# A decoder step on one Trainium2 core: norms between blocks summed tile by tile, a fixed order at the block boundaries, and x loaded in four parts

## Chip, cores and metric

The kernel runs on one core of one Trainium2 chip, as one program. The metric is the device time of one execution in microseconds. A profiled execution gives the trace. Engines are named as in the profile: PE (TensorE), DVE (VectorE), ACT (ScalarE), POOL (GpSimd), SP (SyncE, which only issues transfers here).

## What is computed

One inference step of a trunk of two layers. Layer 1 mixes time by an RWKV-7 recurrence, layer 2 by an RG-LRU; a causal convolutional FFN follows each. There are 256 prompt positions of one sequence and 8 sample positions with states of their own. Each of the four blocks is wrapped in the same way:

```python
h = rms_norm(x, norm_g_in) * (1 + sc) + sh        # sc, sh, gt: from the condition c, by silu(c) @ w_mod
out = mixer_or_ffn(h)
x = x + gt * rms_norm(out, norm_g_out)            # rms_norm: over the 2048 channels
```

After a block, the norm of `out` needs the sum of squares over all 2048 channels of `out`, and the next block's first products need the norm of the new x as well. The returned values are y and the updated states.

## The kernel before

Activations lie with channels on the partitions: 2048 channels are 16 chunks of 128 partitions, by T = 264 columns (256 prompt, 8 sample). `U0` holds x, `U1` a block's output. Weights are streamed from HBM in tiles of 1 MB (`raw`, `rawx`, five buffers), each of two pieces. ACT rounds a piece to its high half `wh` (L434), DVE subtracts to get the low half `wl` (L435); there are four buffers of each. A product is three matmuls (L455 high x high, L456 high x low, L457 low x high); a piece has 24 of them, four column blocks by two chunks by three (`mm_pieces`, L448). `mm_group` (L462) runs the pieces of a group of four column blocks. Between pieces it pumps the adaLN modulation (`wm_pump`, `wm_load`: small products of `w_mod` tiles, L345) as filler on PE.

**Norm of a block's output.** Each column block's result is squared on ACT (L530) and twelve of the sixteen squares are added on POOL into `sqacc`; the last four stay separate in `SqAcc.tail`. After the last product `rstd_of` (L480) multiplies a matrix of constants with `sqacc` and the four tails on PE (L484, five matmuls), ACT takes the root (`sd`, L486), DVE the reciprocal (`rs`, L488).

**Boundary between blocks** (`residual` L539, `residual_and_h` L554, called three times). The residual is a step per pair of chunks, `step(e, j, n)`: an engine multiplies U1 by the reciprocal (`bt`, L549) and adds to U0 (L550). The 8 sample columns of all chunks go in one pair of instructions (L543, L544). From the new U0 the kernel forms `x * (1 + sc)` in a high half `XH` (ACT, L580) and a low half `XL` (DVE, L581); the sample and shift columns are prepared in `xe` (POOL, L568) and cast in one piece (L569, L570). ACT also squares the new x by pairs (`sqb`, L577), DVE adds the pair (L582), PE sums them (`norm(p)`, L586). The first products of the next block, `main(p)` for the eight pairs of chunks p = 0 to 7, run on XH and XL ahead of that norm, which is divided out later. Pairs 0 to 4 have their step on DVE, 5 to 7 (chunks 10, 12, 14) on POOL. The engines' order here is that of the tile framework's scheduler.

**Start.** x comes in one transfer (L326). `NormPipe.push` squares each chunk on ACT and sums it on PE; eight chunks are pushed after the first modulation piece, eight after the second (L751 to L756). Then come the transposed modulation vector, the first h and the projections of the RWKV mixer.

**WKV stage.** The recurrence runs by chunks of 16 positions; its 1749 jobs are issued in the order of a table, `ORDER` (L37), under `manual_schedule`.

**Tail** (L1789 to L1794). The last residual is done in steps on DVE and POOL, then eight output transfers are issued.

Of the kernel before, what the change touches and what calls it, by code (L numbers as in the profile page):

```python
# [8 lines left out]
F32 = mybir.dt.float32  # L9
# [33 lines left out]
v1 2v0 v1 2s2 2w4 p6 p7 b3 p6 2w5 u4 u5 x1 p6 v1 p6 2v0 2v1 2b2 v0 3q0 d4 b3 v1 q0 2b3 2q0 p7 3b3 q0 2p8 2h0
d4 2p7 p6 2h0 q0 p8 h0 3q0 l8 p8 2p6 b4 4s2 p6 3q0 3b3 p7 s4 p7 2v1 d5 2x2 p7 2l9 3q0 2v2 p7 2v1 p7 q0 h0 v1
2v2 a0 q0 o0 2p6 3p7 w7 2o0 2p6 l11 v3 2p7 2q1 v2 d7 q1 v2 4p9 p8 o0 2h0 2s4 2v2 2q1 v2 2b4 b5 o0 2v2 2p8 v3
a1 3o0 l10 h0 p7 v3 2x2 p9 q0 x2 v3 s4 w6 2s4 4o0 p9 3x2 p8 2x2 w6 p8 2q1 2p8 b4 d6 4q1 b4 2g0 s4 2g0 2p9 3g0
u6 w7 u7 v3 2q1 b4 2g0 3q1 s4 g0 v4 b4 2v4 l10 4v3 d6 d7 2w8 2s6 u8 v4 b4 v3 4q1 2g0 2a0 w9 q0 q1 a0 v3 a0 s6
# [241 lines left out]
def build(nc, tc, I, O, dbg=None):  # L289
# [42 lines left out]
    def pv(name, i, n=1):  # L332
# [1487 lines left out]
```

## Time and profile before

| | |
|---|---|
| median of 3 runs | 2849.76 us (2849.45 to 2850.34) |
| the profiled execution's own time | 2848.57 us |
| its span in the trace | 2846.8 us |
| mean granted clock of PE | 0.987 |
| busy: PE, DVE, ACT, POOL | 96%, 62%, 48%, 18% |

Times in the trace count from the start of the span. A granted clock of 1.00 is the higher level of 2.4 GHz. In a timeline each row has the start, the length, the engine, the line, the operation and, in brackets, how long the engine was idle before it and which instruction released it. The stages: start to 40 us, projections to 378, WKV stage to 712, its output product to 813, boundary 1, FFN, boundary 2 from 1670, RG-LRU mixer, boundary 3 from 2021, FFN, tail from 2824.

### The profile page before, as it was taken

Reading aid. Unit: us, or ns where it says so; the run is one execution under the profiler, and the core shown is the slowest. Engines: PE = TensorE matmul, PEld = TensorE weight load, DVE = VectorE, ACT = ScalarE, POOL = GpSimd, SP = SyncE. Lnnn points to the kernel's source line nnn. Section 1 sums busy time; section 2 is a strip of 40 time slices with the busy share of each in tenths; the row PEclk is TensorE's granted clock in tenths of the full one; section 3 lists DMA queues with packets and bytes.
Section 4 is the critical chain, followed back from the end, with each engine's and each line's share of the span. In section 5 each row is a group of like instructions: output and inputs, shape, how many; then the busy total and the mean of one; then the engine's idle time right before and its main releaser. Section 6 shows DMA issues by size and latency. Waiting matters only on the chain.

```text
span 2846.8 us, 61582 instructions
## 1 busy us (share of the span) xinstructions
PE 2740.7 (96%) x25820; PEld 2526.2 (89%) x25820; DVE 1753.7 (62%) x2824; ACT 1358.7 (48%) x2187; POOL 524.4 (18%) x1045
## 2 busy tenths in 40 slices
PE   7999999888999999999999999999999999999997
PEld 6899876665989999999999989999899999999997
DVE  5877776876476535545545579775765455455555
ACT  5333435644455434433434459785554444344444
POOL 2111435553121000000000023332210000000002
PEclk9999999999999999999999999999999999999998
DMA  8777558776766666666666665666666555555552
GB/s 330 288 261 244 185 176 246 241 234 215 276 237 232 257 245 238 252 252 255 247 237 252 256 248 199 253 239 237 237 244 252 207 180 178 178 180 184 183 183 76
DMA packets 146566, 648.48 MB, mean 228 GB/s; under 512 B 41152, under 2 KB 60752, under 8 KB 78064
## 3 DMA queue, kind: packets, MB, share of 16 engines
q1 hardware_dynamic: 145216, 641.25, 62.7%
q8 instruction: 202, 3.31, 0.5%
q0 software_dynamic: 1072, 3.30, 0.4%
q14 instruction: 76, 0.62, 0.1%
HBM read 629.42 MB, written 15.07 MB: 226 GB/s over the span
## 4 chain that ended last, share of the span: by engine, by line
PE 86%; DVE 7%; ACT 2%; DMA 2%; issue 1%; POOL 1%; SPq 0%; DVEq 0%; ACTq 0%; POOLq 0%
PE bk L455 18%; PE bk L456 18%; PE bk L457 18%; PE sq L455 7%; PE sq L456 7%; PE sq L457 7%; PE wm L345 5%; DVE wl L435 1%; PE bk L902 1%; ACT wh L434 1%; DVE bt L549 1%; PE bk L908 1%; PE bk L814 0%; PE sq L814 0%; DVE U L550 0%
## 5 line engine op out<-in xcount | busy, mean ns | idle before, releaser
L435 DVE TENSOR_TENSOR wl<-raw,wh 128x1024 fp32r<-128x1024 f32 x444 | 547.6, 1235 | 495.0 <-ACT wh L434 485.8
L434 ACT CAST wh<-raw 128x1024 fp32r<-128x1024 f32 x444 | 464.5, 1048 | 631.6 <-PE bk L456 428.4
L455 PE MATMUL bk<-AH,wh 128*128 128x264 f32 x2352 | 670.6, 285 | 1.4 <-ACT wh L434 1.4
L457 PE MATMUL bk<-AH,wl 128*128 128x264 f32 x2352 | 669.1, 284 | 1.7 <-DVE wl L435 1.6
L456 PE MATMUL bk<-AL,wh 128*128 128x264 f32 x2352 | 668.6, 284 | 0.8 <-DVE AL L493 0.8
L435 DVE TENSOR_TENSOR wl<-rawx,wh 128x1024 fp32r<-128x1024 f32 x310 | 379.3, 1226 | 331.9 <-ACT wh L434 326.8
L434 ACT CAST wh<-rawx 128x1024 fp32r<-128x1024 f32 x310 | 324.4, 1048 | 452.9 <-PE bk L456 332.7
L455 PE MATMUL bk<-ah,wh 128*128 128x264 f32 x1786 | 514.6, 289 | 9.2 <-ACT ah L492 5.5
L457 PE MATMUL bk<-ah,wl 128*128 128x264 f32 x1786 | 510.6, 286 | 0.5 <-DVE wl L435 0.5
L456 PE MATMUL bk<-al,wh 128*128 128x264 f32 x1786 | 510.6, 286 | 0.0
L455 PEld LDWEIGHTS bk<-AH,wh 128*128 128x128 f32 x2352 | 443.3, 188 | 20.7 <-ACT cv L1560 8.4
L457 PEld LDWEIGHTS bk<-AH,wl 128*128 128x128 f32 x2352 | 441.7, 188 | 2.8 <-DVE wl L435 2.8
L456 PEld LDWEIGHTS bk<-AL,wh 128*128 128x128 f32 x2352 | 442.5, 188 | 1.0 <-DVE AL L493 1.0
L455 PEld LDWEIGHTS bk<-ah,wh 128*128 128x128 f32 x1786 | 337.6, 189 | 27.6 <-ACT wh L434 8.1
L457 PEld LDWEIGHTS bk<-ah,wl 128*128 128x128 f32 x1786 | 338.1, 189 | 1.4 <-DVE wl L435 0.8
L456 PEld LDWEIGHTS bk<-al,wh 128*128 128x128 f32 x1786 | 338.4, 189 | 0.6 <-DVE al L493 0.2
L455 PE MATMUL sq<-AH,wh 128*128 128x264 f32 x1040 | 296.7, 285 | 0.1
L456 PE MATMUL sq<-AL,wh 128*128 128x264 f32 x1040 | 295.6, 284 | 0.0
L457 PE MATMUL sq<-AH,wl 128*128 128x264 f32 x1040 | 295.4, 284 | 0.0
L1553 POOL COPY fgs<-gt 128x10 f32<-128x10 f32 x88 | 53.4, 634 | 1307.5 <-ACT gt L1547 1286.2
L455 PEld LDWEIGHTS sq<-AH,wh 128*128 128x128 f32 x1040 | 196.0, 188 | 9.6 <-ACT cv L1560 3.4
L456 PEld LDWEIGHTS sq<-AL,wh 128*128 128x128 f32 x1040 | 195.7, 188 | 0.0
(469 smaller groups left out, 4501.3 us busy)
## 6 DMA issues: line engine op xcount, KB each, us to landing
raw<-in_wst SPq DMA_DIRECT2D x224, 1024.0 KB, 4.9
rawx<-in_wst SPq DMA_DIRECT2D x157, 1024.0 KB, 4.8
raw<-in_wmr SPq DMA_DIRECT2D x72, 1024.0 KB, 7.6
raw<-in_wmr SPq DMA_DIRECT2D x88, 512.0 KB, 5.5
rawx<-in_wmr SPq DMA_DIRECT2D x44, 1024.0 KB, 8.2
raw<-in_wmq SPq DMA_DIRECT2D x23, 1024.0 KB, 4.9
rawx<-in_wmq SPq DMA_DIRECT2D x9, 1024.0 KB, 4.8
lu<-in_lup SPq DMA_DIRECT2D x32, 128.0 KB, 4.8
```

The source lines that it names most:

```text
L345: PE.matmul(ps[32 * g:32 * g + 32, :cols], cs[:, k0 + kk, :], raw[:, (kk * 4 + g) * cols:(kk * 4 + g + 1) * cols], start=(k0 + kk == 0), s ...
L434: S.copy(wh, t)
L435: V.tensor_sub(wl, t, wh.bitcast(F32))
L455: PE.matmul(ps[:, :n], h[:, kk, sl], xh, start=first and kk == 0, stop=False)
L456: PE.matmul(ps[:, :n], h[:, kk, sl], xl, start=False, stop=False)
L457: PE.matmul(ps[:, :n], l[:, kk, sl], xh, start=False, stop=last and kk == 1)
L549: e.tensor_tensor(t, U1[:, j:j + n, :TP], r1[:, None, :TP].to_broadcast([128, n, TP]), op=mult)
L902: PE.matmul(out[HH[(i + turn) % 2]], lhs[HH[i]], rhs[HH[i]], start=start, stop=stop, skip_group_check=True)
L908: PE.matmul(out[q], lhs(r), rhs[r], start=start, stop=stop, skip_group_check=True)
L1553: G.tensor_copy(gs[:, m], gt[:, TP:])
```

## The change

1. **Norm sums.** `rstd_of` is gone. `SqAcc` gets `begin` (the matmul of `sqacc`) and `add_tail`. In the last group of a block, `begin` is issued ahead of the last piece, and a hook after each column block of that piece squares it; the first two tails are added behind the third and fourth column blocks, so that one norm matmul lies between them. The gating of the last two column blocks (`acc.rest`) is moved behind the reciprocal.
2. **Filler.** In that last group two pieces of modulation filler are pumped ahead of the last piece, not behind it; at the boundary two, and two more after the fixed part.
3. **Boundary.** A fixed order (`manual_schedule`) up to `norm(0)`. The sample columns are split: two chunks on DVE, 14 on POOL; so are `xe` and its casts. Squares, halves and pair sums become calls of their own.
4. **Start.** x in four transfers; all sixteen squares are pushed ahead of the modulation pieces.
5. **Tail.** The eight steps are all on DVE, the sample columns on POOL, and each output transfer is issued behind its step.
6. **`ORDER`**: another order of the same jobs. Its first line was `s0 g0 p0 l0 2p0 p1 3x0 ...`, and is `l0 g0 2p0 s0 x0 g0 2x0 l0 6p0 l1 ...`.

```diff
-    SP.dma_start(U0[:, :, 1:], I["xT"])
+    for j in range(0, 16, 4):
+        SP.dma_start(U0[:, j:j + 4, 1:], I["xT"][:, j:j + 4])
...
+            end = q == nk // 2 - 1
+            if acc and end:
+                acc.begin()
+            mm_pieces(pss, pc, [rhs(2 * q), rhs(2 * q + 1)], q == 0, end, T, hook if end else None)
...
-                elif p == 0:
+                elif p == (2 * pace[0] - 1 if ahead and q >= nk // 2 - 2 else 0):
                     wm_pump(2, False)
-            if ahead and q == nk // 2 - 1:
-                for w in range(ahead):
-                    wm_load(wm_state["i"] + w)
+                    for w in range(ahead):
+                        wm_load(wm_state["i"] + w)
...
+        def begin(s):
+            s.ps = bank()
+            PE.matmul(s.ps[:, :T], onesd, s.acc, start=True, stop=False)
+
+        def add_tail(s, i):
+            PE.matmul(s.ps[:, :T], onesd, s.tail[i], start=False, stop=i == 3)
...
-        parts(0)
-        main(0)
-        step(V, 2, 2)
-        step(G, 12, 2)
-        parts(1)
-        norm(0)
-        step(V, 4, 2)
+        with tc.manual_schedule(engines=MANUAL):
+            step, sample = residual(pool, acc)
+            wm_pump(2, False)
+            wm_load(wm_state["i"])
+            wm_load(wm_state["i"] + 1)
+            sample(V, 0, 2)
+            sample(G, 2, 14)
+            step(V, 0, 2)
+            extra(V, 0, 2)
+            halves(0)
+            main(0)
+            step(V, 2, 2)
+            extra(G, 2, 14)
+            halves(1)
+            squares(0)
+            main(1)
+            pairsum(0)
+            step(V, 4, 2)
+            squares(1)
+            pairsum(1)
+            step(G, 10, 2)
+            step(G, 12, 2)
+            norm(0)
+        wm_pump(2, False)
         parts(2)
-        main(1)
         norm(1)
         step(V, 6, 2)
         step(G, 14, 2)
...
+    for j in range(16):
+        np0.push(U0[:, j, 1:])
     for kp in range(4):
         mod_piece(0, kp)
-        if kp < 2:
-            for j in range(8 * kp, 8 * kp + 8):
-                np0.push(U0[:, j, 1:])
...
+            def hook(m, ps):
+                acc.push(ps[:, :T])
+                if m < 2:
+                    gated(m, ps)
+                else:
+                    acc.rest.append(lambda: gated(m, ps))
+                    acc.add_tail(m - 2)
+
+            if g == 3:
+                with tc.manual_schedule(engines=MANUAL):
+                    mm_group(16, rhs, bgg, 2, acc, hook)
+                    acc.add_tail(2)
+                    acc.add_tail(3)
+                break
...
-    step = residual(bp, acc, 8)
-    for e, j in ((V, 0), (G, 12), (V, 2), (V, 4), (G, 14), (V, 6), (V, 8), (V, 10)):
-        step(e, j, 2)
-    for j in (0, 2, 12, 4, 6, 8, 14, 10):
-        SP.dma_start(O["yT"][:, j:j + 2], U0[:, j:j + 2, 1:])
+    with tc.manual_schedule(engines=MANUAL):
+        step, sample = residual(bp, acc, 8)
+        sample(G, 0, 16)
+        for j in range(0, 16, 2):
+            step(V, j, 2)
+            SP.dma_start(O["yT"][:, j:j + 2], U0[:, j:j + 2, 1:])
```

`mm_group(16, ...)` is the form in the out-projection; the FFN's last group has the same hook with the addition to the partial sums in front.

How the instructions move is shown at boundary 1 (the other two are alike). Line numbers of the changed kernel are its own: L435 and L436 are there the casts wh and wl, L456 to L458 the products, L523 and L526 the norm sums, L547 the reciprocal, L560 and L561 a step, L584 and L585 XH and XL, L579 the squares, L595 the pair sums.

On PE, before, at the end of the out-projection (the last products of a piece, the filler, the norm sums, more filler, and the first product of main(0)):

```order
L455 MATMUL bk<-ah,wh 128x264
L456 MATMUL bk<-al,wh 128x264
L457 MATMUL bk<-ah,wl 128x264
L345 MATMUL wm<-raw,cT 32x512 x8
L484 MATMUL sq<-sqacc,onesd 128x264
L484 MATMUL sq<-sq,onesd 128x264 x4
L345 MATMUL wm<-rawx,cT 32x512 x4
L345 MATMUL wm<-raw,cT 32x512 x12
L455 MATMUL sq<-XH,wh 128x274
L456 MATMUL sq<-XL,wh 128x274
```

Now, ahead of the last piece:

```order
L346 MATMUL wm<-raw,cT 32x512 x8
L523 MATMUL sq<-sqacc,onesd 128x264
L456 MATMUL bk<-ah,wh 128x264
L457 MATMUL bk<-al,wh 128x264
L458 MATMUL bk<-ah,wl 128x264
```

and at the end of that piece:

```order
L456 MATMUL bk<-ah,wh 128x264
L457 MATMUL bk<-al,wh 128x264
L458 MATMUL bk<-ah,wl 128x264
L526 MATMUL sq<-sq,onesd 128x264 x3
L346 MATMUL wm<-rawx,cT 32x512 x4
L346 MATMUL wm<-raw,cT 32x512 x12
L456 MATMUL sq<-XH,wh 128x274
L457 MATMUL sq<-XL,wh 128x274
```

Eight filler matmuls of the program now stand ahead of the last piece, with the sum of `sqacc` behind them; of the four tails three are left behind the last product.

On DVE, before, from the last wl cast ahead of the reciprocal up to the first XL and pair sums (the next wl cast, the one for main(4), stands eleven rows further):

```order
L435 TENSOR_TENSOR wl<-rawx,wh 128x1024
L1509 TENSOR_TENSOR U_10834<-bk,mod_7071 128x8
L488 RECIPROCAL rs_11694<-sd 128x264
L543 TENSOR_TENSOR f_11696<-U_10834,rs_11694 128x128
L549 TENSOR_TENSOR bt<-U_10834,rs_11694 128x512
L544 TENSOR_TENSOR U_78<-U_78,f_11696 128x16x8
L550 TENSOR_TENSOR U_78<-U_78,bt 128x2x256
L549 TENSOR_TENSOR bt<-U_10834,rs_11694 128x512
L570 TENSOR_TENSOR XL<-xe,XH 128x16x18
L550 TENSOR_TENSOR U_78<-U_78,bt 128x2x256
L581 SCALAR_TENSOR_TENSOR XL<-U_78,mod_11379,XH 128x256 x2
L582 TENSOR_TENSOR sqb<-sqb 128x264 x2
```

Now, from XL 0 and 1 (eight rows behind the reciprocal) up to the pair sum ahead of XL 4 and 5:

```order
L585 SCALAR_TENSOR_TENSOR XL<-U_78,mod_11382,XH 128x256 x2
L436 TENSOR_TENSOR wl<-rawx,wh 128x1024
L560 TENSOR_TENSOR bt<-U_10837,rs_11703 128x512
L561 TENSOR_TENSOR U_78<-U_78,bt 128x2x256
L591 TENSOR_TENSOR XL<-xe,XH 128x14x18
L585 SCALAR_TENSOR_TENSOR XL<-U_78,mod_11382,XH 128x256 x2
L436 TENSOR_TENSOR wl<-rawx,wh 128x1024
L595 TENSOR_TENSOR sqb<-sqb 128x264
L560 TENSOR_TENSOR bt<-U_10837,rs_11703 128x512
L436 TENSOR_TENSOR wl<-rawx,wh 128x1024
L561 TENSOR_TENSOR U_78<-U_78,bt 128x2x256
L595 TENSOR_TENSOR sqb<-sqb 128x264
```

Three wl casts, for main(2), main(3) and main(4), now stand between the steps; before, two of them were ahead of the reciprocal.

On ACT, before, from the root to the casts for main(4) and main(5):

```order
L486 ACTIVATE sd<-sq,epsn 128x264
L580 ACTIVATE XH<-U_78,mod_11379 128x256
L569 CAST XH<-xe 128x16x18
L577 ACTIVATE sqb<-U_78 128x528
L580 ACTIVATE XH<-U_78,mod_11379 128x256 x2
L577 ACTIVATE sqb<-U_78 128x528
L580 ACTIVATE XH<-U_78,mod_11379 128x256 x5
L577 ACTIVATE sqb<-U_78 128x528
L580 ACTIVATE XH<-U_78,mod_11379 128x256 x2
L577 ACTIVATE sqb<-U_78 128x528
L580 ACTIVATE XH<-U_78,mod_11379 128x256 x2
L434 CAST wh<-rawx 128x1024 x2
```

Now, from the sample columns' XH:

```order
L590 CAST XH<-xe 128x2x18
L584 ACTIVATE XH<-U_78,mod_11382 128x256 x2
L435 CAST wh<-rawx 128x1024
L590 CAST XH<-xe 128x14x18
L584 ACTIVATE XH<-U_78,mod_11382 128x256 x2
L579 ACTIVATE sqb<-U_78 128x528
L435 CAST wh<-rawx 128x1024
L579 ACTIVATE sqb<-U_78 128x528
L435 CAST wh<-rawx 128x1024 x2
L584 ACTIVATE XH<-U_78,mod_11382 128x256 x3
L579 ACTIVATE sqb<-U_78 128x528
L584 ACTIVATE XH<-U_78,mod_11382 128x256 x5
```

The wh casts for main(2) to main(5) are now ahead of XH 4 and 5, which stand in the last row behind XH 10 to 12; before, XH 4 and 5 were ahead of the casts.

## Rows read from the trace of the kernel before

**Rows 1.** Windows by stage: PE, PEld, DVE, ACT, POOL busy; clock; DMA; GB/s.
```profile
378.00:712.00 334.00, 294.44 (x5876) 209.34 (x5875) 237.21 (x555) 171.53 (x456) 157.52 (x350) 0.96 0.76 235
712.00:2824.00 2112.00, 2089.07 (x16933) 1990.50 (x16933) 1228.71 (x1755) 1032.69 (x1484) 261.87 (x512) 0.99 0.61 224
```

**Rows 2.** Chain of waits, 0 to 45 us: start, length, engine, tile, line.
```profile
1.67 12.45 DMA U<-in_xT
...
25.71 1.28 ACT L511
...
29.24 0.16 DVE wmtt L740
...
33.99 1.25 PE bk L455 x4
```

**Rows 3.** Timeline of PE, start.
```profile
22.74 3.83 PE L506 MATMUL bk<-sq,onesd 128*128 128x264 f32 x16
...
27.39 1.06 PE L345 MATMUL wm<-rawx,cT 128*32 128x128 f32 x32
```

**Rows 4.** Windows of 2 us, start.
```profile
22.00:24.00 2.00, 2.00 (x38) 1.64 (x27) 0.00 (x0) 0.75 (x3) 0.00 (x0) 1.00 1.01 418
```

**Rows 5.** Timeline of PE, boundary 1.
```profile
812.89 0.28 PE L457 MATMUL bk<-ah,wl 128*128 128x264 f32 x1
813.10 1.92 PE L345 MATMUL wm<-raw,cT 128*32 128x512 f32 x16
...
815.51 1.94 PE L484 MATMUL sq<-sq,onesd 128*128 128x264 f32 x8
...
825.37 0.59 PE L455 MATMUL sq<-XH,wh 128*128 128x274 f32 x1 [2.74 <-ACT XH L580]
827.94 0.60 PE L456 MATMUL sq<-XL,wh 128*128 128x274 f32 x1 [1.97 <-DVE XL L581]
...
832.82 0.48 PE L455 MATMUL sq<-XH,wh 128*128 128x274 f32 x1
...
836.76 0.48 PE L455 MATMUL sq<-XH,wh 128*128 128x274 f32 x1
```

**Rows 6.** Windows of 4 us, boundary 1, and their sum.
```profile
824.00:828.00 4.00, 0.66 (x2) 0.35 (x2) 4.00 (x5) 2.20 (x5) 2.86 (x2) 0.58 1.01 426
...
sum 24.00, PE 17.89 PEld 13.84 DVE 21.96 ACT 12.09 POOL 9.51; mean PE 2.98 PEld 2.31 DVE 3.66 ACT 2.02 POOL 1.59
```

**Rows 7.** Timeline of DVE, boundary 1.
```profile
814.21 1.23 DVE L435 TENSOR_TENSOR wl<-rawx,wh 128x1024 fp32r<-128x1024 f32 x1 [0.76 <-PE wm L345]
...
818.00 1.80 DVE L488 RECIPROCAL rs<-sd 128x264 f32<-128x264 f32 x1 [2.49 <-ACT sd L486]
...
820.05 1.75 DVE L549 TENSOR_TENSOR bt<-U,rs 128x512 f32<-128x512 f32 x1
...
822.91 0.68 DVE L550 TENSOR_TENSOR U<-U,bt 128x512 f32<-128x512 f32 x1
...
832.09 1.51 DVE L581 SCALAR_TENSOR_TENSOR XL<-U,mod,XH 128x256 fp32r<-128x256 f32 x1
...
834.87 0.87 DVE L581 SCALAR_TENSOR_TENSOR XL<-U,mod,XH 128x256 fp32r<-128x256 f32 x2
```

**Rows 8.** Timeline of POOL, boundary 1.
```profile
819.88 1.37 POOL L549 TENSOR_TENSOR bt<-U,rs 128x512 f32<-128x512 f32 x1 [28.50 <-DVE rs L488]
```

**Rows 9.** Timeline of ACT, boundary 1.
```profile
833.82 0.89 ACT L580 ACTIVATE XH<-U,mod 128x256 fp32r<-128x256 f32 x2
834.61 1.04 ACT L434 CAST wh<-rawx 128x1024 fp32r<-128x1024 f32 x1
```

**Rows 10.** Timeline of PE, boundary 2.
```profile
1685.42 0.60 PE L456 MATMUL sq<-XL,wh 128*128 128x274 f32 x1 [1.97 <-DVE XL L581]
```

**Rows 11.** Timeline of DVE, tail.
```profile
2829.66 1.80 DVE L488 RECIPROCAL rs<-sd 128x264 f32<-128x264 f32 x1 [1.29 <-ACT sd L486]
...
2842.75 0.69 DVE L550 TENSOR_TENSOR U<-U,bt 128x512 f32<-128x512 f32 x1
```

More of the change, by code (lines that the diff above doesn't have):

```diff
@@ L43 @@
[L43 to L47, printed above, removed]
@@ L446, in build, with mm_pieces @@
     ws = Stream()
-    def mm_pieces(pss, pc, rhs2, first, last, n=T):
+    def mm_pieces(pss, pc, rhs2, first, last, n=T, hook=None):
         h, l = pc
@@ L539, in residual, with sample @@
     def residual(pool, acc, nb=2):
-        r1 = rstd_of(pool, [acc.acc] + acc.tail, "rs1")
+        sd = pool([128, T], F32, "sd", 1)
+        S.activation(sd, acc.ps[:, :T], AF.Sqrt, bias=epsn)
+        r1 = pool([128, T], F32, "rs1", 1)
+        V.reciprocal(r1, sd)
+        for f in acc.rest:
+            f()
         f8 = pool([128, 16, 8], F32, "f8", 1)
-        V.tensor_tensor(f8, U1[:, :, TP:], r1[:, None, TP:].to_broadcast([128, 16, 8]), op=mult)
-        V.tensor_tensor(U0[:, :, TP + 1:], U0[:, :, TP + 1:], f8, op=add)
+        def sample(e, j, n):
+            x = U0[:, j:j + n, TP + 1:]
+            e.tensor_tensor(f8[:, j:j + n], U1[:, j:j + n, TP:], r1[:, None, TP:].to_broadcast([128, n, 8]), op=mult)
+            e.tensor_tensor(x, x, f8[:, j:j + n], op=add)
         def step(e, j, n):
@@ L550, in step @@
             e.tensor_tensor(x, x, t, op=add)
-        return step
+        return step, sample
     def residual_and_h(acc, sc, sh, AH, AL):
@@ L581, in parts, with extra, pairsum @@
                 V.scalar_tensor_tensor(XL[:, j, :TP], x, sc[:, j, 0:1], XH[:, j, :TP].bitcast(F32), op0=mult, op1=sub)
-            V.tensor_tensor(q[:, 0], q[:, 0], q[:, 1], op=add)
-            sqs[p] = q
+        def extra(e, j, n):
+            x = slice(j, j + n)
+            e.tensor_tensor(xe[:, x, :8], U0[:, x, TP + 1:], sc[:, x, 1:], op=mult)
+            S.copy(XH[:, x, TP:], xe[:, x])
+            V.tensor_sub(XL[:, x, TP:], xe[:, x], XH[:, x, TP:].bitcast(F32))
+        def pairsum(p):
+            q = sqs[p]
+            V.tensor_tensor(q[:, 0], q[:, 0], q[:, 1], op=add)
+        def parts(p):
+            squares(p)
+            halves(p)
+            pairsum(p)
+        pss = [bank() for _ in range(4)]
+        ms = bank()
         def norm(p):
@@ L1506, in out_proj @@
             for m in range(4):
[L1507 to L1509 removed]
+                gated(m, pss[m])
         return acc
@@ L1572, in ffn, with gated, hook @@
                     S.activation(junk, acc.acc[:, :1], AF.Sqrt)
-                pss = mm_group(b - a, lambda k: hid[k], None, 2 if last and g == 3 else 0)
+                def gated(m):
+                    u = U1[:, 12 + m]
+                    S.activation(u[:, :TP], u[:, :TP], AF.Copy, scale=gate[:, 12 + m, 0:1])
+                    V.tensor_tensor(u[:, TP:], u[:, TP:], gate[:, 12 + m, 1:], op=mult)
+                def hook(m, ps):
+                    u = U1[:, 12 + m]
+                    V.tensor_tensor(u, u, ps[:, :T], op=add)
+                    acc.push(u)
+                    if m < 2:
+                        gated(m)
+                    else:
+                        acc.rest.append(lambda: gated(m))
+                        acc.add_tail(m - 2)
+                if last and g == 3:
+                    with tc.manual_schedule(engines=MANUAL):
+                        mm_group(b - a, lambda k: hid[k], None, 2, acc, hook)
+                        acc.add_tail(2)
+                        acc.add_tail(3)
+                    break
+                pss = mm_group(b - a, lambda k: hid[k])
                 for m in range(4):
```

115 lines of the change are left out of this document (54 added, 61 removed).

## The prediction

> **What bounds the kernel now.** I read the busy times by stage first, then the waits of TensorE (PE), then the timelines of the stretches that the change touches. The windows by stage show that from 712 us to 2824 us PE is busy 2089.07 of 2112.00 us, and in the stage before it, the WKV recurrence, 294.44 of 334.00 us [rows 1]. So a reordering off PE's path can gain nothing; it can only close PE's gaps or open new ones. The gaps that this change can reach are four: the start, up to the first weight product; the three boundaries between blocks, where the kernel normalises a block's output and prepares the next input; the last boundary, which is the tail; and the 39.6 us that PE idles in the WKV stage.
>
> At the start the chain of waits shows one transfer of x lasting 12.45 us, later the Sqrt table, then the modulation's transpose at 29.24 and the first product at 33.99 [rows 2]. PE's timeline shows why the middle takes so long: the norm's 32 matmul records are interleaved with the modulation products, the last 16 taking 3.83 us from 22.74, so that the fourth modulation piece runs only at 27.39 [rows 3].
>
> At boundary 1 the last product starts at 812.89, the norm sums end around 817.4, the first product of the new block starts at 825.37 and the second, which needs the low half XL, at 827.94 [rows 5]. VectorE (DVE) finishes the reciprocal at 818.00 + 1.80 = 819.80 [rows 7]; I call this moment R and count from it. Product groups have 24 matmuls each; group main(2) starts at 836.76 = R + 16.96, and PE no longer waits there [rows 5]. Boundary 2 has the same wait of 1.97 us for XL [rows 10], and boundary 3 the same pattern.
>
> **The norm sum: no earlier R.** The five norm matmuls take 2.4 us in all (two records each, from 815.02 to 817.45), so 0.48 each. Two of the five now run before the end of the last group, and the square of the third column block lies under the products of the fourth. But the modulation filler of 16 records, 1.9 us, which stood between the last product and the sums, is moved ahead of the last piece too [rows 5]. PE therefore ends its last product 1.94 + 0.96 = 2.90 us later than before, and what follows is a square (0.39), the last tail, the root (0.48) and the reciprocal (1.80): with the hand-overs about 3.55 us. R falls 6.45 us after the old end of the products, against 819.80 - 813.17 = 6.63 before. Gain 0.2 us per boundary. Two gated copies move behind the root on ScalarE (ACT) and hide under the reciprocal.
>
> **From R to main(2): the new fixed order.** main(0) gets what it needs sooner: DVE now does a sample part of two chunks, one step, and goes straight to XL 0 and 1, so main(0) starts near R + 4.7, not R + 8.1. That is worth something only if main(1) and main(2) follow, and I price main(2), since PE runs without a wait from there.
> DVE's own work up to XL 4 and 5, at durations that nothing disturbs (0.65 for an instruction of a step, 0.43 for an XL, 1.23 for a wl cast [rows 7], and about 0.42 for a pair sum): before, 0.6 for the sample part, 0.45 for its XL, eight step instructions 5.2, seven XL 3.0 and three pair sums 1.26, 10.5 us in all. It was there at 834.87 + 0.87 = R + 15.9 [rows 7]: 5.4 us were lost while GpSimd (POOL) worked. The rows show the loss: a 0.65 instruction took 1.75 at 820.05, beside a POOL step of 1.37 [rows 8], and an XL took 1.51 at 832.09 [rows 7].
> After: copies and sample part 0.7, seven step instructions 4.55, six XL 2.6, the sample's xe and XL 0.75, three pair sums 1.26, and three wl casts 3.7: 13.5 us. The casts are the difference. Before, the casts for main(2) and main(3) were done ahead of R (the last at 814.21, when DVE waited anyway [rows 7]); the new order puts them, and main(4)'s, between the steps. POOL still has three steps (10, 12, 14) and a sample part of 14 chunks, so I keep the loss at 5.4 us and add 0.6 us for waiting on ACT's first XH and wh: XL 5 at R + 19.5, main(2) from about R + 19.2. Against R + 16.96 that is 2.2 us later, 2.0 with the earlier R.
> ACT gives a second, lower bound. Its casts for main(4) and main(5) wait until PE has read main(0) and main(1), and XH 4 and 5 stand behind them, and behind XH 10 to 12, which wait for POOL. With 1.04 for a cast and 0.45 for an XH [rows 9], main(2) comes some 3.8 us (a cast, five XH, a square of 0.55) after main(1) ends, at R + 4.7 + 4.4 + 3.0 = R + 12.1: R + 15.9. DVE's bound is later and decides.
> PE idles some 5 us ahead of main(2). Gaps of 2.74 and 1.97 us [rows 5] came with a granted clock of 0.58 from 824 to 828 [rows 6], so mostly the lower of the two levels, 1.2 GHz: main(0) with one norm took 832.82 - 827.94 = 4.88 us, main(1) with two took 3.94 [rows 5]; less 0.48 a norm, 4.4 against 3.0, so 1.4 us were lost, say 1.5. I add it once more, since the new gap is longer than each of those. **Per boundary +3.5 us**; bounds -2.7 (rival 1) and +7.5 (rival 2). The moved POOL sample part, the DMA issues of two modulation tiles and the filler's two later pieces I cost at nothing: DVE's steps cover them, and PE's queue has wm records ready before main(0). Without that cover the filler costs its 1.9 us.
> The Trainium skill (SBUF — State Buffer, section "SBUF: two separate sides") says that VectorE with two SBUF inputs and GpSimd hold a shared port pair exclusively, the loser blocking for the whole instruction; the trace agrees, with 1.75 us for what takes 0.65 alone.
>
> **The start.** x comes in four loads, and its squares and sums stand ahead of the modulation products. The last byte of x lands no sooner than 14.14; then four squares and their sums are left, and table load, root and reciprocal end near 20, off the path. The end is now set by the modulation tiles: four of 1 MB behind x at 418 GB/s [rows 4] take 9.9 us, up to 24.0; the last products, 1.06 [rows 3], end near 25.1, the transpose starts there in place of 29.24, and the 4.75 us from there to the first product stay [rows 2]. **-4.1 us**; bounds -5.5 (transfers overlap better) and -2.5 (the added loads delay the tiles by 1.6 us, as chosen).
> The Trainium skill (SBUF — State Buffer, "The DMA setup-cost knee") advises the largest single transfer, since each pays about 2 us; by it three more loads would take back the start's gain. The DMA share beside several loads in flight was 1.01 [rows 4], which speaks against that.
>
> **WKV stage.** The table is another order of the same 1749 jobs, and two ACT table loads (1.28 us each, as the one at 25.71 [rows 2]) fall away. No row says what PE gains or loses in its 39.6 us of gaps. I take 0; bounds -5 and +5, an eighth of the gaps.
> **Tail.** R moves 0.4 us later against the old end of the products, as the sums are no longer preceded by filler; eight DVE steps of 1.2 us and two disturbed starts take 11.4 us, where DVE and POOL together took from 2831.47 to 2843.44 [rows 11]. **-0.2 us**; bounds -1 and +0.6. Outputs leave step by step, but the last still ends the kernel.
> **Sum.** 3 x 3.5 - 4.1 + 0 - 0.2 = +6.2 us on the profiled execution's 2848.57: 2854.8. That execution is 1.19 us under the runs' median, 2849.76, so the forecast in medians is 2856.0.
>
> **Rivals.** 1. *POOL's interference falls into DVE's waits for ACT.* Then DVE is not the bound, PE has no long gap, and its clock stays up: main(0) and main(1) take 3.0 us each from R + 4.7, main(2) follows 3.8 us later at R + 14.5: -2.5, with R -2.7. Three times, with the start and the tail: -12.4, 2837.4: faster. For it: DVE does wait at two points. Against: from 816 to 840 DVE was busy for 21.96 of 24 us [rows 6], so it has little waiting to give.
> 2. *Every POOL instruction costs DVE its full length.* Six step instructions at 1.4 us [rows 8] and short ones of 1 us in all, 9.4 us in place of 5.4: XL 5 at R + 23.5, +7.5 per boundary, +18.2 in all: 2868.0. For it: the 1.75 and 1.51 above show losses of 1.1. Against: before, 9.51 us of POOL [rows 6] cost 5.4. By the skill's rule of the exclusive lock this is the case to expect.
> 3. *R really comes earlier*, because the filler would have waited for its tiles: -1.9 per boundary, +0.5 in all: 2850.3.
> 4. *The WKV order decides*, by more than 5 us either way: 2848 or 2864.
>
> **How the numbers follow.** Forecast 45%, rival 1 26%, rival 2 15%, rival 3 8%, rival 4 6%. A change of 0.2%, 5.7 us, is about what a measurement can tell. The forecast lies on that edge: 26 of its 45 are slower, 19 the same. Rival 1 gives 22 faster and 4 the same, rival 2 14 slower and 1 the same, rival 3 8 the same, rival 4 3, 2 and 1. Together 25% faster, 34% the same, 41% slower. The forecast's own range is 2849 to 2862; to hold 8 in 10 it reaches to the nearer half of rivals 1 and 2: 2838 to 2866.
>
> **What would show it.** First product near 29.9; R 6.4 us after the old place of the products' end; main(0) near R + 4.7; a wait of PE for XL or XH ahead of main(2) of 4 us or more; wl casts between DVE's steps. The prediction is wrong if PE runs from main(0) to main(7) without a wait, or if its gaps in the WKV stage change by over 5 us.

## The result, and the profile after

The changed kernel is slower: a median of 2873.39 us (2870.21 to 2879.2, 4 runs) against 2849.61 us (2848.56 to 2850.34, 4 runs), ratio 1.0088 with a 95% interval of 1.0072 to 1.0104. The forecast had the likelier sign, slower, but 2856.0 us and an upper end of 2866 us. The span grew from 2846.8 to 2871.5 us, and the mean granted clock of PE fell from 0.987 to 0.983.

To see where the 24.7 us lie I mark the same work in both traces: each has 754 weight casts (`wh`), so the distance from the k-th to a later one is the length of a stage. Start and projections end with cast 88, the WKV stage with 92, boundary 1 lies in 120 to 152, boundary 2 in 372 to 412, boundary 3 in 472 to 512. The first row is the changed kernel; the others are the experiments below. Times are differences in us from the profile of before; the ratio is that of the timed runs.

| kernel | ratio (95%) | start | WKV | b1 | b2 | b3 | tail |
|---|---|---|---|---|---|---|---|
| the change | 1.0088 (1.0072–1.0104) | -3.5 | +8.9 | +6.2 | +8.2 | +6.2 | -0.7 |
| e1 old table | 1.0060 (1.0045–1.0075) | -2.3 | +2.5 | +6.3 | +8.2 | +6.7 | -0.7 |
| e2 new table alone | 1.0043 (1.0032–1.0054) | -1.2 | +16.3 | +0.7 | +0.2 | +0.8 | 0.0 |
| e3 start alone | 0.9996 (0.9987–1.0006) | -4.8 | -1.4 | -0.2 | +0.8 | +1.1 | -0.2 |
| e4 free boundary | 1.0026 (1.0016–1.0036) | -1.5 | +4.0 | +2.3 | +5.7 | +2.7 | -0.7 |
| e5 sums alone | 1.0016 (1.0005–1.0026) | -1.4 | +1.6 | +2.2 | +1.8 | +1.9 | +0.5 |
| e6 early casts | 1.0030 (1.0020–1.0040) | -2.4 | +1.1 | +2.3 | +4.2 | +3.3 | -0.7 |
| e7 POOL later | 1.0047 (1.0031–1.0064) | -1.9 | -0.1 | +4.4 | +7.8 | +5.4 | -0.7 |
| e8 reordered | 1.0034 (1.0024–1.0045) | -1.7 | +5.8 | +3.6 | +4.9 | +3.8 | -0.7 |
| e9 pair sums on PE | 1.0048 (1.0034–1.0062) | -1.8 | -1.8 | +4.7 | +5.5 | +4.2 | 0.0 |
| e10 e9, start, tail | 1.0035 (1.0021–1.0048) | -3.6 | +6.0 | +7.8 | +5.9 | +4.4 | -1.1 |
| e11 e6, sums on PE | 1.0034 (1.0021–1.0047) | -2.9 | +5.4 | +4.0 | +5.8 | +3.0 | -0.7 |
| e12 sums by four | 1.0036 (1.0023–1.0049) | -0.8 | +2.2 | +2.4 | +3.9 | +2.7 | 0.0 |
| e13 one sum | 1.0013 (1.0004–1.0023) | -1.4 | +3.0 | +0.9 | 0.0 | +1.8 | 0.0 |
| e14 e12, start, tail | 1.0020 (1.0011–1.0030) | -2.0 | +1.1 | +2.5 | +2.5 | +2.1 | -1.0 |
| e15 start, tail | 0.9995 (0.9986–1.0004) | | | | | | |

e15's profiled execution took 6769.31 us, more than twice every other one (last section), so its ratio is taken without that execution and its row has no stages.

A profile is one execution, so the table has noise to be read first: with the old table the WKV column runs from -1.8 to +6.0, +2.3 on average, and kernels whose start is as before show -0.8 to -1.8 in the start column. The column of a boundary is steadier, but in e12 and e14 another 1.0 us of boundary 2 falls behind cast 412, so that it cost them 4.9 and 3.5 us.

**Boundaries: 20.6 of the 24.7 us.** PE's timeline at boundary 1, with R = 824.72 from the first row of DVE's timeline below:

```profile
820.75 0.28 PE L458 MATMUL bk<-ah,wl 128*128 128x264 f32 x1
820.87 1.50 PE L526 MATMUL sq<-sq,onesd 128*128 128x264 f32 x6
...
827.86 0.39 PE L456 MATMUL sq<-XH,wh 128*128 128x274 f32 x1 [1.76 <-ACT XH L584]
828.38 0.39 PE L457 MATMUL sq<-XL,wh 128*128 128x274 f32 x1
...
838.55 0.68 PE L606 MATMUL bk<-sqb,onesd 128*128 128x264 f32 x2 [0.86 <-DVE sqb L595]
...
841.24 0.68 PE L606 MATMUL bk<-sqb,onesd 128*128 128x264 f32 x2 [2.00 <-DVE sqb L595]
...
844.16 1.25 PE L606 MATMUL bk<-sqb,onesd 128*128 128x264 f32 x2 [1.76 <-DVE sqb L595]
844.83 0.80 PE L457 MATMUL sq<-XL,wh 128*128 128x274 f32 x1
```

main(0) is there at R + 3.1 and has its first product with XL at R + 3.7, where before that stood at 827.94, R + 8.1 [rows 5]. But PE then stands still for the pair sums (`sqb`) three times, 4.6 us, and goes on without a wait only in main(2), whose first product with XL is at R + 20.1. Before, that product stood at R + 17.3:

```profile
837.08 0.29 PE L456 MATMUL sq<-XL,wh 128*128 128x274 f32 x1
```

DVE's timeline shows what it did in that time (columns as in [rows 7]):

```profile
822.92 1.80 DVE L547 RECIPROCAL rs<-sd 128x264 f32<-128x264 f32 x1 [2.79 <-ACT sd L545]
...
829.18 1.23 DVE L436 TENSOR_TENSOR wl<-rawx,wh 128x1024 fp32r<-128x1024 f32 x1 [0.45 <-ACT wh L435]
...
832.31 2.52 DVE L585 SCALAR_TENSOR_TENSOR XL<-U,mod,XH 128x256 fp32r<-128x256 f32 x2 [0.24 <-ACT XH L584]
834.75 2.31 DVE L436 TENSOR_TENSOR wl<-rawx,wh 128x1024 fp32r<-128x1024 f32 x1
836.98 1.42 DVE L595 TENSOR_TENSOR sqb<-sqb 128x264 f32<-128x264 f32 x1
...
838.93 1.21 DVE L436 TENSOR_TENSOR wl<-rawx,wh 128x1024 fp32r<-128x1024 f32 x1
...
841.01 1.76 DVE L560 TENSOR_TENSOR bt<-U,rs 128x512 f32<-128x512 f32 x1
842.70 1.40 DVE L595 TENSOR_TENSOR sqb<-sqb 128x264 f32<-128x264 f32 x1
844.03 0.87 DVE L585 SCALAR_TENSOR_TENSOR XL<-U,mod,XH 128x256 fp32r<-128x256 f32 x2
```

Three casts (`wl`) stand between the steps, as forecast, and the steps beside POOL are stretched: two XL take 2.52 us, which take 0.87 alone (last row, as in [rows 7]). From these two XL on DVE has no wait until XL 4 and 5 are done. POOL's rows of the same time:

```profile
831.88 1.34 POOL L560 TENSOR_TENSOR bt<-U,rs 128x512 f32<-128x512 f32 x1 [4.82 <-DVE U L561]
833.29 1.25 POOL L561 TENSOR_TENSOR U<-U,bt 128x512 f32<-128x512 f32 x1
...
842.30 1.51 POOL L561 TENSOR_TENSOR U<-U,bt 128x512 f32<-128x512 f32 x1
```

ACT's timeline shows its queue:

```profile
834.59 1.04 ACT L435 CAST wh<-rawx 128x1024 fp32r<-128x1024 f32 x1
837.66 1.05 ACT L435 CAST wh<-rawx 128x1024 fp32r<-128x1024 f32 x1 [2.03 <-PE bk L457]
838.61 1.30 ACT L584 ACTIVATE XH<-U,mod 128x256 fp32r<-128x256 f32 x3
...
849.97 1.05 ACT L435 CAST wh<-rawx 128x1024 fp32r<-128x1024 f32 x1 [2.94 <-PE bk L457]
```

A cast that waits for PE to read an older piece holds up the XH behind it. But up to XL 4 and 5 it is DVE's own queue that PE waits for, the three casts and the stretched instructions: of R + 19.3, where XL 4 begins, DVE spent only 1.25 us waiting, 0.45 of it for a `wh`. And the clock falls a second time, which before it did not. By windows, the second of them at a granted 0.54, so nearly all at the lower level:

```profile
836.00:844.00 8.00, 3.54 (x20) 2.36 (x18) 8.00 (x8) 4.25 (x9) 4.89 (x3) 0.92 0.37 131
844.00:850.00 6.00, 5.84 (x25) 5.64 (x26) 5.76 (x12) 2.22 (x6) 0.00 (x0) 0.54 0.00 0
```

5.84 us at 0.54 cost 2.7. With main(2) later by 20.1 - 17.3 = 2.8 us and two later waits for `wl` in the next block (1.01 us in all, against 0.24) that is 6.3 us; the table has +6.2.

**WKV: +8.9.** In the stretch that answers to [rows 1], PE idles 41.4 us instead of 39.6, and at a granted 0.94 it loses 17.8 us to the clock instead of 11.8 (busy time times the missing share of the clock, an estimate). The two windows do not hold the same work, as the changed kernel is 3.5 us ahead when the stage begins. From cast 88 to cast 92, in the sums of ten windows each, before and then now, PE idles 44.3 us instead of 40.6, and by these windows the clock costs 18.0 instead of 12.0:

```profile
sum 369.70, PE 329.13 PEld 239.18 DVE 264.99 ACT 177.94 POOL 177.52; mean PE 32.91 PEld 23.92 DVE 26.50 ACT 17.79 POOL 17.75
```
```profile
sum 378.70, PE 334.42 PEld 244.38 DVE 267.48 ACT 174.86 POOL 171.47; mean PE 33.44 PEld 24.44 DVE 26.75 ACT 17.49 POOL 17.15
```

These are the rows of that stretch and of the stage's last fifth:

```profile
378.00:716.00 338.00, 296.61 (x5857) 212.41 (x5857) 236.39 (x547) 166.27 (x451) 151.56 (x351) 0.94 0.73 229
...
641.10:716.80 75.70, 61.53 (x1224) 42.14 (x1220) 46.29 (x111) 29.52 (x91) 15.64 (x20) 0.84 0.59 194
```

The same fifth of before, for comparison:

```profile
637.50:711.40 73.90, 63.11 (x1348) 43.59 (x1334) 45.42 (x111) 32.95 (x101) 25.45 (x48) 0.91 0.67 218
```

There PE idles 14.2 us instead of 10.8, and the clock costs 9.8 instead of 5.7: 7.5 us in the last fifth alone. One profile against another could be chance here, but idle time and clock together take 14.5 to 18.4 us of this fifth in all fourteen profiles with the old table, and 24.1 and 25.6 us in the two with the new (the change and e2). POOL has 15.64 us of work left there instead of 25.45. That the new order has too little work beside its last chain fits this, but no run tests it.

**Start: first product at 31.03** instead of 33.99 [rows 2]. PE's timeline, and the window from 31 to 37 us:

```profile
31.03 0.59 PE L456 MATMUL bk<-ah,wh 128*128 128x264 f32 x1 [5.52 <-ACT wh L435]
...
33.68 0.59 PE L458 MATMUL bk<-ah,wl 128*128 128x264 f32 x1 [0.97 <-DVE wl L436]
```
```profile
31.00:37.00 6.00, 5.00 (x21) 4.70 (x22) 6.00 (x8) 4.68 (x9) 2.67 (x4) 0.50 0.87 328
```

Before, the first products also followed a wait of 5.5 us and also ran at 0.50:

```profile
34.00:39.00 5.00, 5.00 (x22) 4.78 (x22) 5.00 (x7) 2.25 (x3) 4.55 (x4) 0.50 0.49 170
```

So the clock is no lower than before and isn't what takes the gain. New is the wait of 0.97 us for `wl`: it stands in all ten profiles with the new start, in none with the old one. Over these ten the start column has -2.7 on average; the five with the old start (e2, e5, e9, e12, e13) have -1.3. So the new start is worth some 1.3 us, though the first product comes 2.7 us sooner on average.

### The profile page after: what moved, and what is told of

It is laid out like the page before. It is cut to its first block, busy times and chain, and to the rows that moved or that the text cites. A ratio compares the mean times of both kernels' runs of the same rounds, so it can differ in the third digit from the quotient of the medians.

```text
span 2871.5 us, 61601 instructions
## 1 busy us (share of the span) xinstructions
PE 2760.5 (96%) x25820; PEld 2536.9 (88%) x25820; DVE 1754.7 (61%) x2832; ACT 1356.1 (47%) x2188; POOL 520.7 (18%) x1049
## 5 line engine op out<-in xcount | busy, mean ns | idle before, releaser
L436 DVE TENSOR_TENSOR wl<-raw,wh 128x1024 fp32r<-128x1024 f32 x444 | 547.0, 1233 | 493.4 <-ACT wh L435 485.0
L435 ACT CAST wh<-raw 128x1024 fp32r<-128x1024 f32 x444 | 464.7, 1047 | 625.6 <-PE bk L457 424.3
L458 PE MATMUL bk<-AH,wl 128*128 128x264 f32 x2352 | 669.4, 285 | 5.3 <-DVE wl L436 5.1
L456 PE MATMUL bk<-AH,wh 128*128 128x264 f32 x2352 | 670.6, 285 | 0.0
L436 DVE TENSOR_TENSOR wl<-rawx,wh 128x1024 fp32r<-128x1024 f32 x310 | 382.2, 1235 | 332.7 <-ACT wh L435 328.4
L435 ACT CAST wh<-rawx 128x1024 fp32r<-128x1024 f32 x310 | 324.5, 1048 | 449.9 <-PE bk L457 334.4
L456 PE MATMUL bk<-ah,wh 128*128 128x264 f32 x1786 | 515.8, 289 | 10.1 <-ACT wh L435 10.1
L458 PE MATMUL bk<-ah,wl 128*128 128x264 f32 x1786 | 510.2, 286 | 1.4 <-DVE wl L436 1.4
L456 PEld LDWEIGHTS bk<-AH,wh 128*128 128x128 f32 x2352 | 443.3, 188 | 18.5 <-ACT cv L1614 9.2
L458 PEld LDWEIGHTS bk<-AH,wl 128*128 128x128 f32 x2352 | 441.6, 188 | 7.4 <-DVE wl L436 7.4
L456 PEld LDWEIGHTS bk<-ah,wh 128*128 128x128 f32 x1786 | 337.9, 189 | 28.5 <-ACT wh L435 15.0
L458 PEld LDWEIGHTS bk<-ah,wl 128*128 128x128 f32 x1786 | 337.5, 189 | 2.2 <-DVE wl L436 2.0
L456 PE MATMUL sq<-AH,wh 128*128 128x264 f32 x1040 | 296.8, 286 | 0.1
L458 PE MATMUL sq<-AH,wl 128*128 128x264 f32 x1040 | 295.4, 284 | 0.0
L456 PEld LDWEIGHTS sq<-AH,wh 128*128 128x128 f32 x1040 | 196.0, 188 | 10.4 <-ACT wh L435 3.4
```

The lines of the kernel that those rows point to most:

```text
L435: S.copy(wh, t)
L436: V.tensor_sub(wl, t, wh.bitcast(F32))
L456: PE.matmul(ps[:, :n], h[:, kk, sl], xh, start=first and kk == 0, stop=False)
L458: PE.matmul(ps[:, :n], l[:, kk, sl], xh, start=False, stop=last and kk == 1)
```

## Experiments

**e1 to e4: which part costs what.** e1 is the change with the old order of the WKV jobs, e2 the kernel before with the new order, e3 the kernel before with the new start, e4 is e1 with the boundary's order left to the scheduler.

```diff
# e1, in the change:            ORDER of before
# e2, in the kernel before:     ORDER of the change
# e3, in the kernel before
-    SP.dma_start(U0[:, :, 1:], I["xT"])
+    for j in range(0, 16, 4):
+        SP.dma_start(U0[:, j:j + 4, 1:], I["xT"][:, j:j + 4])
...
# e4, in e1
-        with tc.manual_schedule(engines=MANUAL):
+        if True:
             step, sample = residual(pool, acc)
```

> The changed kernel with the old table of the WKV stage. Theory T (the new table itself costs some 9 us: the cast after the WKV stage comes 5.4 us later than before, the one ahead of it 3.5 us sooner): 2864.5 us, and that cast about 3.5 us sooner than before. Rival (the old table would lose as much here, since the earlier start or the shifted filler upsets the stage): 2873 us, cast still late. By a third theory (run-to-run clock losses in the stage) it falls in between and the runs scatter by several us.

> The kernel before with nothing changed but the table. Theory T: 2858.5 us, all of the loss between 378 and 712 us. Rival (the table costs only together with the earlier start): 2849.6 us.

> The kernel before with x in four loads and its squares first, nothing else. Theory: first product at 31.0 in place of 34.0 us, the gain kept to the end of the stage: 2846.4 us. Rival (the gain is lost in the WKV stage, which waits for something else): first product at 31.0, 2849.6 us. If the projections' casts keep the 3.5 us seen at the end of that stage: 2846.

> The changed kernel with the old table and with the fixed order taken away from the boundaries' front part (the framework's scheduler orders the same instructions there; the norm sums inside the last piece and the split sample columns stay). Theory F (the fixed order costs: casts between the steps): the wl casts for main(2) and main(3) stand ahead of the reciprocal again, each boundary is back near its old length, and the time is 2846 us (2843 to 2849). Rival S (the split sample columns, POOL's three steps in one stretch, or the norm sums in the last piece cost): 2858 to 2865 us.

The table alone costs 13.0 us (2862.88 against 2849.88) in the kernel before, and 5.7 us (2873.39 against 2867.66; 8.0 by the ratios) in the change; why it costs less there is open. The last fifth of the stage shows that it goes with the table, not with the rest: e2 has the row of the changed kernel, e1 that of before. First e2, then e1:

```profile
649.30:726.50 77.20, 61.52 (x1224) 42.13 (x1220) 46.45 (x111) 29.43 (x92) 15.23 (x20) 0.84 0.59 190
```
```profile
637.10:711.60 74.50, 62.67 (x1316) 42.79 (x1312) 44.59 (x109) 32.47 (x101) 24.03 (x45) 0.93 0.63 210
```

The new start alone gives no measurable difference. Without the fixed order (e4, 2857.84 us: theory F fell) the boundaries cost 10.7 us in all instead of 21.2 (e1): the order written out by hand is half of their loss.

**e5 to e8: what at the boundary.** e5 is the kernel before with the norm sums and the filler moved as in the change, and nothing else. In e1, e6 makes the casts for the next pieces ahead of the root, e7 puts POOL's steps 10 and 12 later, and e8 does e6 and puts POOL's steps behind the norms and main(2) ahead of them.

```diff
# e6, in e1
                 acc.begin()
+                ws.split_to(ws.i + 2)
...
+        ws.split_to(ws.i + 3)
         sd = pool([128, T], F32, "sd", 1)
# e7, in e1
-            step(G, 10, 2)
-            step(G, 12, 2)
             norm(0)
...
         step(V, 6, 2)
+        step(G, 10, 2)
+        step(G, 12, 2)
```

> The kernel before with the norm sums in the last piece and the shifted filler, nothing else (old table, old start, old boundary order, old tail). Theory (the sums gain nothing and cost nothing, since the filler and two of the five norm matmuls only change sides): the reciprocal ends within 0.5 us of its old distance to the products, each boundary keeps its length to 1 us, 2850 us. Rival (they cost some 2.5 us per boundary, which is what is left in the kernel whose fixed order was taken away): 2857 us.

> The changed kernel with the old table, and with the casts for main(2) and main(3) put ahead of the reciprocal again; the rest of the fixed order stays. Theory D (VectorE's casts between the steps delay XL 4 and 5): 2.46 us less for VectorE behind the reciprocal, some 0.6 us more ahead of it, so each boundary is 1.9 us shorter than with the old table alone, in all 5.5 us: 2862 us. Rival A (ScalarE's queue decides, or PE's norms that stand ahead of main(2)): under 0.5 us per boundary, 2867 us.

> The changed kernel with the old table, and with POOL's steps 10 and 12 written behind step 6 of VectorE, so that POOL gets its buffers later and VectorE's step 6 no longer waits for POOL's step 12. Theory P (POOL's steps stretch VectorE's instructions ahead of XL 4 and 5 by about 4 us): XL 4 stands some 15 us behind the reciprocal in place of 19, each boundary is 3 to 4 us shorter, 2857 us. Rival D (the casts alone are the loss): under 1 us per boundary, 2866 us.

> Both together, and XL 4 and 5 with main(2) written ahead of the pair sums, of step 6 and of POOL's steps. Theories D and P together: VectorE's own work up to XL 5 falls from 13.5 to about 8 us, main(2) follows main(1) without a wait near 12 to 13 us behind the reciprocal, each boundary is 3 us shorter than in the kernel before, 9 shorter than with the old table alone: 2841 us. Rival (the wait moves to a later pair, behind POOL's steps, or the clock's drop takes it): 2850 us or more.

The sums alone cost 5.9 us in three boundaries (4.5 us by the medians, 2855.86 against 2851.37): they are not the small gain of the forecast. The other 4.8 of the 10.7 us in e4 must lie in the split sample columns and the calls of their own; no run takes them apart. In e5's boundary 1 the last product ends at 816.32, and ACT has a cast ahead of the last square:

```profile
816.24 1.04 ACT L434 CAST wh<-rawx 128x1024 fp32r<-128x1024 f32 x1 [0.29 <-PE bk L456]
817.19 0.38 ACT L532 ACTIVATE sq<-bk 128x264 f32<-128x264 f32 x1
```

Before, the filler of 1.92 us and the sums behind the last product [rows 5] covered such work; ahead of the last piece they cover nothing. PE's first product with XL shows what is left: it starts 829.82 - 816.32 = 13.5 us after the last product, 16.4 with the 2.90 us that were moved ahead, against 14.8 before [rows 5].

```profile
829.82 0.60 PE L456 MATMUL sq<-XL,wh 128*128 128x274 f32 x1
```

The early casts bring the boundaries from 21.2 to 9.8, as much as the scheduler's order does, and twice what theory D gave (11.4 us instead of 5.5). But e6 moves two things at once, the casts on ACT and those on DVE. ACT's waits for PE from 820 to 862 us fall; first of the change, then of e6 (engine, what waits, for what: us in total, times, longest):

```profile
ACT wh L435 <- PE bk L457: 6.3, 3, 2.9
```
```profile
ACT wh L435 <- PE bk L457: 1.3, 2, 1.1
```

DVE's rows in e6 show what reached PE at boundary 1:

```profile
818.25 1.80 DVE L549 RECIPROCAL rs<-sd 128x264 f32<-128x264 f32 x1 [0.84 <-ACT sd L547]
...
835.39 0.87 DVE L587 SCALAR_TENSOR_TENSOR XL<-U,mod,XH 128x256 fp32r<-128x256 f32 x2
```

XL 4 begins 15.3 us behind R in e6, 19.3 in the change and in e1, as the three `wl` casts, 4.75 us in the change, no longer stand in between. PE's waits for `sqb` fell from 4.6 to 2.65 us, and the clock's second fall stayed away. In neither kernel does DVE wait between the second pair of XL and XL 4, so no run shows that ACT's waits cost anything by themselves. e6 pays 1.2 us of its gain in R, which comes 4.86 instead of 3.69 us after the last product, as a cast stands ahead of the last square again. POOL's steps put later (e7) give 3.7 us in all, 1.9 of them at boundary 1: moving POOL's interference gives the smaller part. The two together (e8) do not add up, 12.3 us, where 2841 us had been expected and 2861.95 came: PE waits later, for the pair sums and for XL of the later pairs. By windows of 2 us the clock took 4.5 us from PE's busy time at boundary 1 in e8 and 4.7 in e4, as in the change (4.5; before 2.1, e6 3.1).

**e9 to e11: is DVE the bound?** Between R and the first AH of the next block DVE was busy 37.9 of 38 us in the kernel before, so I took it for the bound of a boundary. e9 takes work off it: the pair sums go to PE.

```diff
# e9, in the kernel before
-            V.tensor_tensor(q[:, 0], q[:, 0], q[:, 1], op=add)
...
-            PE.matmul(ms[:, :T], onesd, sqs[p][:, 0], start=(p == 0), stop=(p == 7))
+            PE.matmul(ms[:, :T], onesd, sqs[p][:, 0], start=(p == 0), stop=False)
+            PE.matmul(ms[:, :T], onesd, sqs[p][:, 1], start=False, stop=(p == 7))
# e10: e9 with the new start and tail; e11: the same edit in e6
```

> The kernel before, with one edit: the pair sums of the boundary's squares (a DVE addition for each of eight pairs, 0.42 us) are gone, and the norm of a pair is two matmuls on PE in place of one. DVE does 3.4 us less per boundary, PE 3.8 us more. If DVE's work between the reciprocal and the first AH of the new block bounds that stretch (DVE was busy 37.9 of 38 us there), each boundary gets 2 to 3 us shorter, 2842. If DVE's business there is slack and PE decides once main(0) has begun, each gets 1 to 3.8 us longer, 2853 to 2861.

> The kernel before with the parts of the change that gained (x in four loads with its squares first, and the tail on DVE alone with each output issued behind its step), and the pair sums on PE. By the theory that DVE bounds the boundary: -2 at the start, -0.7 at the tail, -2 to -3 at each boundary, 2838 to 2842. If DVE does not bound it: 2850 to 2858.

> The change with the old order of the WKV jobs and the casts pulled ahead of the reciprocal (the run e6), and the pair sums on PE as well. By the theory that DVE bounds the boundary, each gets 2 to 3 us shorter than in e6: 2851 to 2854. If ACT's queue (XH behind the casts that wait for PE) bounds it, the boundaries stay as in e6: 2858 to 2862.

The theory fell: each boundary got 4.2 to 5.5 us longer, a little more than the 3.8 us of PE work that was added. Ten us inside boundary 1, before and then e9 (columns as in [rows 1]: after the length PE, PEld, DVE):

```profile
838.00:848.00 10.00, 10.00 (x74) 9.67 (x73) 10.00 (x17) 6.33 (x11) 0.00 (x0) 1.00 0.35 111
```
```profile
838.00:848.00 10.00, 10.00 (x67) 9.38 (x66) 4.67 (x5) 3.56 (x5) 0.28 (x1) 1.00 0.41 155
```

DVE is relieved to 4.67 us, and it buys nothing: PE is busy for all ten in both. A DVE that is always busy only had work that it could as well do later. e11 goes the same way, with 12.8 us at the boundaries against 9.8 in e6, though that is far less than the PE work that was added, and e10 misses by 20 us; why its boundary 1 lost 3.1 us more than e9's is open.

**e12 to e15: is it PE alone, and does any version beat both?** These take norm matmuls off PE, at the price of DVE work.

```diff
# e12, in the kernel before
-            V.tensor_tensor(q[:, 0], q[:, 0], q[:, 1], op=add)
+            if p % 2:
+                V.tensor_tensor(q, q, sqs[p - 1], op=add)
+                V.tensor_tensor(q[:, 0], q[:, 0], q[:, 1], op=add)
...
-            PE.matmul(ms[:, :T], onesd, sqs[p][:, 0], start=(p == 0), stop=(p == 7))
+            if p % 2:
+                PE.matmul(ms[:, :T], onesd, sqs[p][:, 0], start=(p == 1), stop=(p == 7))
# e13: the same over all eight pairs, one matmul
# e14: e12 with the new start and tail; e15: the kernel before with the new start and tail
```

> The kernel before, with one edit: DVE adds the squares of two pairs before PE sums them, so that a boundary has four norm matmuls in place of eight: PE does 1.9 us less, DVE 0.9 us more. If PE's own work bounds the boundary from main(1) on (the run with pair sums on PE says so), each gets 2 to 2.5 us shorter, 2842 to 2845. If DVE bounds it, each gets 0 to 1 us longer, 2850 to 2854.

> The kernel before, with one edit: DVE adds the squares of all eight pairs, and PE sums them in one matmul in place of eight: PE does 3.4 us less per boundary, DVE 1.6 us more, and the norm has its sum only after the last pair. If PE bounds the boundary, each gets 3 to 4 us shorter, 2838 to 2842. If the norm's chain (last pair, root, reciprocal) becomes the bound, or DVE is it, -1 to +2 each, 2847 to 2857.

> The kernel before with quad sums, x in four loads with its squares first, and the tail on DVE alone with each output issued behind its step. If PE bounds the boundary: -6 to -7 at the boundaries, -1 to -2 at the start, -0.7 at the tail, 2840 to 2843. If DVE bounds it: 2848 to 2853.

> The kernel before with only the two parts of the change that gained in their stages: x in four loads with its squares first, and the tail on DVE alone with each output issued behind its step. If these gains stand alone: -1.5 to -2.5 at the start, -0.7 to -1 at the tail, boundaries as before, 2846 to 2848. If the start's gain is given back in the stages behind it: 2849 to 2851.

PE alone is not the bound either. In e12 the first AH does come 1.35 us sooner after the last product of the old block (42.97 against 44.32 us), but PE then waits for casts in the next block, 2.4 us where it was 0.24:

```profile
864.67 0.39 PE L457 MATMUL bk<-AH,wl 128*128 128x264 f32 x1 [1.10 <-DVE wl L435]
...
868.57 0.39 PE L457 MATMUL bk<-AH,wl 128*128 128x264 f32 x1 [0.35 <-DVE wl L435]
...
880.95 0.39 PE L455 MATMUL bk<-AH,wh 128*128 128x264 f32 x1 [0.95 <-ACT wh L434]
```

These waits take back the 1.35 us and 0.8 us more; the rest of the +2.4 I can't place. e12 and e14 (2860.46 and 2856.14 us) came out above both of their forecasts. e13 takes 3.4 us off PE and stays within 2 us of before at each boundary; there PE waits for the first AH, which follows the norm's chain:

```profile
858.12 0.39 PE L455 MATMUL bk<-AH,wh 128*128 128x264 f32 x1 [1.27 <-ACT AH L492]
```

So in the kernel before PE's products and the DVE and ACT work behind them end almost together: more on PE is paid in full, and less on PE at DVE's expense comes back as a wait, for casts one block later in e12, for AH in e13. e15, the parts that gained, is the kernel before within the measurement (0.9995, 0.9986 to 1.0004). No version tried here is measurably faster than the kernel before.

## Why the prediction was right or wrong

- **"No row says what PE gains or loses in its gaps. I take 0"** for the WKV stage: the first step that failed. It is +8.9 in the profile, where the thirteen experiments with the old table have +2.3 on average; by medians the table costs 5.7 us in the change and 13.0 alone. Rival 4, with 6%, named this term, and its bound of 5 us was too narrow, though the boundaries lost more than the table. The bound counted an eighth of the gaps, and left out that the gaps take the clock with them, which was the larger part (some 6.0 us, beside 3.7 us of idle time).
- **"Per boundary +3.5 us"**: the second step; right in sign and mechanism, wrong in its sizes, 20.6 us in three instead of 10.5. At boundary 1 main(2) came 2.8 us later instead of 2.0, the clock cost 2.7 instead of 1.5, and 0.8 us of waits for casts in the next block were not in the sum at all. The terms one by one: R at 3.69 us after the last product, or 6.59 against the old place, was forecast as 6.45 and gave 0.04 instead of 0.2. At boundary 2 a DVE addition stands between the last product and the last square; with the filler gone nothing covers it, and R came 1.3 us late (R at 1689.77, 5.02 us after the last product; 7.92 against the 6.63 of before):

```profile
1684.79 0.43 DVE L1636 TENSOR_TENSOR U<-U,bk 128x264 f32<-128x264 f32 x1 [0.21 <-PE bk L458]
1687.97 1.80 DVE L547 RECIPROCAL rs<-sd 128x264 f32<-128x264 f32 x1 [2.75 <-ACT sd L545]
```

  main(0) came at R + 3.1, forecast R + 4.7, and main(2) at R + 20.1, forecast R + 19.2; PE's wait ahead of it was the 4 us and more that the text asked for, but for the pair sums, which the fixed order puts ahead of it, and not for XL or XH.
- **"DVE's bound is later and decides"**: right. XL 5 was done at 844.90, R + 20.2, forecast R + 19.5, and the third pair sum, which PE takes ahead of it, at 844.10; DVE's waits on the way were 1.25 us in all, forecast 0.6. The ACT queue, the bound 3.3 us lower, did not reach PE there.
- **POOL's loss kept at 5.4 us**: right. Five rows ran beside POOL, the pair of XL, a `wl`, a `bt` and two pair sums, and lost 1.65, 1.09, 1.08, 1.00 and 0.98 us, 5.8 in all. Rival 2 (2868.0 us) came nearest in time by luck: it had 9.4 us, and the excess stood in for the terms above. The Trainium skill (SBUF — State Buffer, "SBUF: two separate sides") has the loser block for the whole instruction of the other engine. The trace agrees: the second XL ends at 834.83, 0.29 us after the POOL instruction that began ahead of it (834.54), and the pair sum of 842.70 ends 0.29 us after POOL's of 842.30. DVE loses what is left of the POOL instruction when it comes to it, not its full length.
- **"-4.1 us" at the start**: the first product came 2.96 us sooner, and about 1.3 us were kept by the average over the profiles. The transpose came at 26.32, forecast 25.1, as PE waited 1.17 and 1.42 us for modulation tiles (the bound of -2.5 had them late by 1.6), and 4.71 us lie from there to the first product, as said. What failed is the step that took the first product's gain for the stage's: the products behind it wait 0.97 us for `wl`. The Trainium skill's advice of the largest single transfer (SBUF — State Buffer, "The DMA setup-cost knee") isn't borne out: the first square of x began at 7.69 us, while the single load before landed at 14.12 [rows 2], and e3 with its four loads is not measurably slower (0.9996).
- **Tail -0.2**: -0.7, and -0.7 to -1.1 in all the kernels that have it.

With the measured terms the sum is 6.2 + 8.2 + 6.2 - 3.5 + 8.9 - 0.7 = +25.3, against a span longer by 24.7; the -0.6 lies between the columns.

## What to carry to other kernels

Starting the first product of a stage sooner is worth less than it seems unless everything that its successors need comes sooner too; count from the point from which PE runs without a wait, and put no work that can be done earlier, here the casts, into an engine's queue ahead of what PE waits for. An engine that is busy all the time is not thereby the bound: take work off it, or give the other one more, before believing it. And price a new order of a stage with gaps by the clock as well as by the gaps, with a range at least as wide as the gaps.

## What the runs showed of the hardware

The clock's part is larger than I had expected: at boundary 1 three waits of 4.6 us in all, with short matmuls between them, stood ahead of 6 us at 0.54; at the start a wait of 5.5 us stood ahead of products at 0.50 in both kernels. And one execution of e15 took 6769.31 us where its other eleven took 2846.97 to 2853.15: the granted clock was 1.00 throughout, but each product's record is 539 ns long, where before the same row has 285, and PE is busy 99% of the span. The profile shows no cause.

The row, in the columns of the page's groups (busy, mean ns of one, idle before):

```profile
L456 PE MATMUL bk<-AH,wh 128*128 128x264 f32 x2352 | 1268.1, 539 | 0.0
```
